# Start offsets of the on-chip tiles of a hybrid encoder block

## The chip, the cores and the metric

The kernel runs on one core of a Trainium2 chip. Its time is that of one execution on the device, in microseconds (us). The times shown are medians of several runs. A profile is a recording of one execution: for each engine of the core, what it executed and when. The engines are TensorE (PE in the profile; its weight loads are PEld), VectorE (DVE), ScalarE (ACT), GpSimd (POOL) and SyncE (SP), which here issues transfers.

## The reference

The reference is one encoder layer on 1,024 tokens of width 1,024, in float32:

```python
h   = x + concat[windowed_attention, bidirectional_gated_deltanet](RMSNorm(x) @ w_in) @ w_out
h   = h + square(relu(RMSNorm(h) @ w_ffn_in)) @ w_ffn_out
out = RMSNorm_final(h)
```

`w_in` has 2,832 columns: queries, keys and values of an attention with 8 query heads and 2 key heads of width 64 and a window of 128 tokens to each side, and queries, keys, values, gate and decay inputs of a gated DeltaNet with 4 heads of width 128, run forwards and backwards. The DeltaNet's queries, keys and values pass first through a centred convolution over 5 tokens and a SiLU. The feed-forward part has 4,096 inner columns.

## The kernel before

**Matmuls.** Large products are made of 128x512 matmuls: a 128x128 block of weights (the stationary operand) is loaded, and 512 columns (the moving operand) stream past it into one bank of PSUM. Each float32 operand is split into a rounded float32r part and the rest, and `mm3` (L122 to L126) issues three matmuls for each block: rounded by rounded, rounded by rest, rest by rounded. Lines 124, 125 and 126 are thus the three kinds of nearly all the matmuls. `split` (L116) makes the two parts, a cast on ScalarE (L119) and a subtraction on GpSimd or VectorE (L120).

**Stages.** The normalised input is transposed on TensorE and split into `pg` tiles. Then come eleven pairs of column blocks of `w_in` (`pair`, L263, with `gemm`, L257): weights in `wh` and `wl` tiles, moving operands in `pg`. The convolution reads raw projections from an `sc` tile (`proj_conv`, L380): 1,024 columns with two zero columns at each end. Beside the projections run the preparation and elimination of the DeltaNet's chunk matrices on VectorE. Then attention, the scan over chunks (`scan`, L768, small float32 matmuls in L797) and the output product (`out_gemm`, L869) are woven together. In `out_gemm` the weights are `pt` tiles and the moving operand is half a `w_out` row block, in `wh` and `wl` for three of the eight row blocks and in `pg` for five.

The feed-forward part computes block products with seven multiplications in place of eight. In the first product (`pair_products`, L1089, 16 groups of 7 products of 12 matmuls) the weights lie in `wh`, `wl` and `sc`, by a table (L1014), and the moving operands in `pg`. Its results go to memory from `pt` tiles (`sd`, L1077) and are read back into `pg` tiles (L1152). In the second product (`second_products`, L1178, four groups of seven steps, each of four banks of 12 matmuls) both operands are halves of `pg` tiles.

**Order.** Generators weighed against each other (`weave`, L55) fix the order of the program's instructions, and each engine executes its own in that order. Waits between engines come from the tiles: a tile that is given out anew waits for the last reader of its buffer.

**Where tiles lie.** A tile takes the same range of bytes in each of the 128 partitions. One pool, `const`, holds single tiles, and a second, `pool`, holds tags, each with its count of buffers (L88 to L110): 28 `pg`, 4 `sc`, 4 `wr`, 3 `wh`, 3 `wl` of 4,096 bytes (`sc` 4,112, because of the convolution's tile) and 12 `pt` of 2,048, and beside them the small tiles of `small`. `const` is opened first, so `pool` begins behind it, at whatever byte the constants end. In the program as built, the first free byte is 16,512 and each buffer takes a multiple of 32 bytes. `const` ends and `sc` begins at 23,648. The offsets from a multiple of 512 are then: `sc` 96, 128, 160 and 192 (its buffers are 4,128 bytes apart), `pg` and `wr` 224, `pt`, `wh` and `wl` 96 (small tiles of the tag `sm` lie in between). The last byte used is about 226,300.

Of the kernel before, what the change touches and what calls it, by code (L numbers as in the profile page):

```python
# [9 lines left out]
F32 = mybir.dt.float32  # L10
# [6 lines left out]
P = 128  # L17
SEQ = 1024
D = 1024
NT = SEQ // P  # L20
NK = D // P
HALF = 512
GH = 4
# [54 lines left out]
class Block:  # L78
# [28 lines left out]
        return self.buf("pt", 12, shape, dt)  # L107

    def small(self, shape, bufs=12, tag="sm", dt=F32):
        return self.buf(tag, bufs, shape, dt)  # L110

    def ps(self, tag, shape=(P, HALF)):
        return self.psum.tile(list(shape), F32, name=self.name(tag), tag=tag, bufs=4)
# [38 lines left out]
    def setup2(self):  # L152
        nc, io, c = self.nc, self.io, self.const
        t = lambda name, shape, dt=F32: c.tile(list(shape), dt, name=name)
        ones = t("ones", (P, P))
        nc.gpsimd.memset(ones, 1.0)
        self.ones = ones
        self.tri = []
        for d, (cm, step) in enumerate(((-1, 1), (1, -1))):
            u = t(f"tri{d}", (P, P))  # L160
            nc.gpsimd.affine_select(out=u, in_=ones, pattern=[[step, P]], compare_op=ALU.is_ge, fill=0.0,
                                    base=0, channel_multiplier=cm)
            self.tri.append(u)
        self.identb = t("identb", (P, P), BF16)
        nc.gpsimd.tensor_copy(out=self.identb, in_=self.ident)
        self.maskb = []
        for d in range(2):
            m = t(f"maskb{d}", (P, P), BF16)
            nc.gpsimd.tensor_scalar(out=m, in0=self.tri[d], scalar1=-1.0, scalar2=-NEG, op0=ALU.add, op1=ALU.mult)
            self.maskb.append(m)  # L170
        self.selb, self.zero = t("selb", (P, 16), BF16), t("zero", (P, 1))
        nc.gpsimd.memset(self.zero, 0.0)
        nc.gpsimd.tensor_tensor(out=self.selb, in0=self.ident[:, 0:16], in1=self.ident[:, 16:32], op=ALU.add)
        nc.gpsimd.tensor_tensor(out=self.selb, in0=self.selb, in1=self.ident[:, 32:48], op=ALU.add)
        self.dtb = t("dtb", (P, 8))
        nc.sync.dma_start(out=self.dtb, in_=io["gdn_dt_bias"].rearrange("o d h -> o (d h)").to_broadcast([P, 8]))
        self.alog = t("alog", (P, 8))
        nc.sync.dma_start(out=self.alog, in_=io["gdn_a_log"].rearrange("o d h -> o (d h)").to_broadcast([P, 8]))
        self.nsink = t("nsink", (P, 8))
        nc.sync.dma_start(out=self.nsink, in_=io["attn_sink"].to_broadcast([P, 8]))  # L180
        nc.gpsimd.tensor_scalar(out=self.nsink, in0=self.nsink, scalar1=-1.0, scalar2=None, op0=ALU.mult)
        self.ssk = t("ssk", (P, GH, NT))
        self.irk = t("irk", (P, GH, NT))
        self.rk2 = t("rk2", (P, GH, NT))
        self.ssq = t("ssq", (P, GH, NT))


# [192 lines left out]
    def proj_conv(self, c0, kind, raws=None):  # L380

        nc = self.nc
        for p in range(2):
            if raws is None:
                raws = self.load_w(self.w_cols(self.io["w_in"][0], c0 + 256 * p, 256))
            bufs = []
            for i, half, ps in self.pair(raws):
                if half == 0:
                    raw = self.sc((P, SEQ + 4))
                    nc.gpsimd.memset(raw[:, 0:2], 0.0)  # L390
                    nc.gpsimd.memset(raw[:, SEQ + 2:SEQ + 4], 0.0)
                    bufs.append(raw)
                raw = bufs[i]
                nc.scalar.copy(out=raw[:, 2 + half * HALF:2 + (half + 1) * HALF], in_=ps)
                yield 5.2
                if half == 1:
                    h = 2 * p + i
                    ct = {"q": 0, "k": 4, "v": 8}[kind] + h
                    out = None if kind == "v" else self.pg()
                    out = self.conv_silu(ct, raw, out)  # L400
                    getattr(self, "head_" + kind)(h, out)
            raws = None
# [832 lines left out]
    def build(self):  # L1235
        tc, nc = self.tc, self.nc
        with (
            tc.tile_pool(name="const", bufs=1) as self.const,
            tc.tile_pool(name="pool", bufs=1) as self.pool,
            tc.tile_pool(name="psum", bufs=1, space=bass.MemoryType.PSUM) as self.psum,  # L1240
            tc.tile_pool(name="dram", bufs=1, space=bass.MemoryType.DRAM) as dram,
        ):
            d = lambda name, shape: dram.tile(list(shape), F32, name=name)
            self.biasd = d("biasd", (8, 32, 512))[:]
            self.hd, self.sd = d("hd", (NT, P, D))[:], d("sd", (DFF // 256, 7, P, HALF))[:]
            self.gcd = dram.tile([3, 64, P], BF16, name="gcd")[:]
            self.zd, self.mad = d("zd", (GH, P, SEQ))[:], d("mad", (NT, P, HALF))[:]
            self.qad = d("qad", (2, 4, P, SEQ))[:]
            self.ktd, self.qtd = d("ktd", (GH, P, SEQ))[:], d("qtd", (GH, P, SEQ))[:]
            self.kvd = d("kvd", (NT, P, 2, GH, P))[:]  # L1250
            self.pd, self.atd = d("pd", (NT, P, 2, GH, P))[:], d("atd", (NT, P, 2, GH, P))[:]
            self.phases()
# [125 lines left out]
```

## Time and profile before

| | us |
|---|---|
| median of 3 runs | 1258.15 |
| lowest and highest | 1256.77 and 1258.52 |
| the profiled execution, span from first to last instruction | 1253.3 |

The profile gives no other time of the profiled execution than its span; the runs' times contain also what lies before its first and after its last instruction.

How to read its rows: in the page's groups, "L124 PE MATMUL psA<-pg,wh 128*128 128x512 f32 x416 | 167.6, 404" is line 124 on TensorE, writing `psA` from `pg` and `wh` (the two operands are not told apart by their order), 416 times, 167.6 us in all and 404 ns on average; then the idle time ahead of them and what ended it. Ends of matmuls in the records are modelled and overlap the next one's start, so the step from start to start is the time that one costs. The timeline gives start, duration, engine, line, operation and operands; neighbours of one kind are sometimes merged, with their count. Lists of transfers end in the size of one and the median time in us from issue to landing.

### The profile page before, as it was taken

How to read it: one execution, taken by the hardware profiler on the slowest of the kernel's cores; microseconds unless marked ns; L12 is line 12 of the kernel's file. 1: busy time of each engine (PE TensorE's matmuls, PEld its weight loads, DVE VectorE, ACT ScalarE, POOL GpSimd, SP SyncE). 2: the span in 40 equal slices, each digit the busy share in tenths (PEclk: the TensorE clock that was granted, in tenths of full speed). 3: DMA queues.
4: the chain of work that ended last, by engine and by line, in shares of the span. 5: the costliest groups of instructions: out<-in, count | busy, mean ns of one | idle time of the engine just before them, and what ended most of it. 6: DMA issues, size and time to landing. Idle time of an engine off the chain costs nothing.

```text
span 1253.3 us, 18527 instructions
## 1 busy us (share of the span) xinstructions
PE 1191.6 (95%) x6482; PEld 967.2 (77%) x6482; DVE 854.9 (68%) x1528; ACT 621.4 (50%) x1347; POOL 580.3 (46%) x488
## 2 busy tenths in 40 slices
PE   7999999899789989998999999999999999999997
PEld 5778777677568868877788888888777888888885
DVE  5667667982389986676655454544668797886976
ACT  6455688335485752125464554545545434444343
POOL 5354211362432433144573534535445665655595
PEclk9999999899889999998999999999999999999999
DMA  7134344441956678122234344443678624434323
GB/s 239 52 121 133 101 171 140 139 126 40 223 168 158 190 216 296 60 84 85 84 131 159 132 151 143 154 159 134 223 280 280 223 85 167 151 121 148 95 90 135
DMA packets 121630, 187.62 MB, mean 150 GB/s; under 512 B 11043, under 2 KB 64416, under 8 KB 121537
## 3 DMA queue, kind: packets, MB, share of 16 engines
q1 hardware_dynamic: 96708, 152.58, 37.9%
q10 hardware_dynamic: 16381, 29.67, 6.3%
q0 software_dynamic: 8448, 4.20, 1.9%
q8 instruction: 51, 0.84, 0.3%
q14 instruction: 42, 0.34, 0.1%
HBM read 122.39 MB, written 63.49 MB: 148 GB/s over the span
## 4 chain that ended last, share of the span: by engine, by line
PE 49%; DVE 6%; DMA 3%; issue 2%; POOL 1%; ACT 1%; ACTq 0%; POOLq 0%; DVEq 0%; SPq 0%
PE psA L124 8%; PE psA L125 8%; PE psA L126 8%; PE psB L126 7%; PE psB L125 7%; PE psB L124 7%; DMA pg<-sd 3%; PE psB L797 2%; DVE pg L1154 1%; DVE pt L1163 1%; DVE wr L1166 1%; PE psB L209 1%; DVE pg L1199 1%; DMA sd<-pt 0%; DVE wr L1161 0%
## 5 line engine op out<-in xcount | busy, mean ns | idle before, releaser
L124 PE MATMUL psA<-pg,wh 128*128 128x512 f32 x416 | 167.6, 404 | 2.1 <-ACT pt L458 2.1
L126 PE MATMUL psA<-pg,wl 128*128 128x512 f32 x416 | 166.9, 401 | 0.0
L125 PE MATMUL psA<-pg,wh 128*128 128x512 f32 x416 | 166.5, 400 | 0.0
L120 POOL TENSOR_TENSOR wl<-wr,wh 128x512 fp32r<-128x512 f32 x44 | 70.2, 1618 | 154.0 <-ACT wh L119 153.9
L1154 DVE TENSOR_TENSOR pg<-pg 128x512 fp32r<-128x512 f32 x112 | 122.7, 1127 | 18.8 <-ACT pg L1153 18.6
L120 POOL TENSOR_TENSOR wh<-wr,wh 128x512 fp32r<-128x512 f32 x32 | 47.9, 1518 | 131.5 <-ACT wh L119 131.5
L1071 ACT ACTIVATE pt<-pt 128x512 f32<-128x512 f32 x64 | 40.4, 632 | 122.7 <-DVE pt L1061 122.7
L125 PE MATMUL psA<-pg,pg 128*128 128x512 f32 x256 | 99.7, 391 | 0.5 <-POOL pg L120 0.5
L124 PE MATMUL psA<-pg,pg 128*128 128x512 f32 x256 | 99.0, 391 | 1.0 <-DVE pg L1199 1.0
L126 PE MATMUL psA<-pg,pg 128*128 128x512 f32 x256 | 99.7, 389 | 0.0
L120 POOL TENSOR_TENSOR pg<-wr,pg 128x512 fp32r<-128x512 f32 x48 | 73.4, 1560 | 51.0 <-ACT pg L119 51.0
L124 PEld LDWEIGHTS psA<-pg,wh 128*128 128x128 f32 x416 | 79.2, 190 | 21.3 <-ACT pt L458 2.4
L125 PEld LDWEIGHTS psA<-pg,wh 128*128 128x128 f32 x416 | 79.3, 191 | 19.7 <-issue 0.9
L126 PEld LDWEIGHTS psA<-pg,wl 128*128 128x128 f32 x416 | 79.1, 190 | 18.6
L1153 ACT CAST pg<-pg 128x512 fp32r<-128x512 f32 x112 | 67.2, 620 | 41.3 <-DMA pg<-sd 31.0
L126 PE MATMUL psB<-pg,pg 128*128 128x512 f32 x192 | 75.0, 390 | 1.3 <-DVE pg L1154 1.3
L125 PE MATMUL psB<-pg,pg 128*128 128x512 f32 x192 | 75.0, 391 | 0.8 <-POOL pg L120 0.7
L124 PE MATMUL psB<-pg,pg 128*128 128x512 f32 x192 | 74.7, 390 | 0.4 <-ACT pg L1153 0.4
L119 ACT CAST wh<-wr 128x512 fp32r<-128x512 f32 x76 | 43.6, 623 | 45.5 <-PE psA L125 24.8
L1061 DVE TENSOR_TENSOR pt<-psB,pt 128x512 f32<-128x512 f32 x39 | 26.9, 689 | 55.1 <-PE psB L126 30.1
L1061 DVE TENSOR_TENSOR pt<-psA,pt 128x512 f32<-128x512 f32 x39 | 26.8, 689 | 55.0 <-PE psA L126 39.5
L124 PEld LDWEIGHTS psA<-pg,pg 128*128 128x128 f32 x256 | 48.0, 188 | 12.6 <-DVE pg L1199 2.3
(385 smaller groups left out, 3307.7 us busy)
## 6 DMA issues: line engine op xcount, KB each, us to landing
sd<-pt ACTq DMA_DIRECT2D x112, 256.0 KB, 2.2
pg<-sd SPq DMA_DIRECT2D x112, 256.0 KB, 2.9
wr<-in_w_ffn_in SPq DMA_DIRECT2D x32, 512.0 KB, 3.8
wr<-in_w_in SPq DMA_DIRECT2D x22, 512.0 KB, 4.8
pg<-in_x SPq DMA_DIRECT2D x16, 512.0 KB, 5.4
wr<-in_w_ffn_out SPq DMA_DIRECT2D x16, 512.0 KB, 4.8
sc<-kvd SPq DMA_DIRECT2D x14, 512.0 KB, 4.1
kvd<-pt SPq DMA_DIRECT2D x16, 256.0 KB, 2.8
```

Source lines behind the costliest of these rows:

```text
L119: nc.scalar.copy(out=h, in_=raw)
L120: (eng or nc.gpsimd).tensor_tensor(out=l, in0=raw, in1=h.bitcast(F32), op=ALU.subtract)
L124: nc.tensor.matmul(ps, wh, xh, start=first, stop=False, skip_group_check=onto)
L125: nc.tensor.matmul(ps, wh, xl, start=False, stop=False, skip_group_check=onto)
L126: nc.tensor.matmul(ps, wl, xh, start=False, stop=last, skip_group_check=onto)
L209: self.nc.tensor.transpose(ps[:, i * P:(i + 1) * P], row[:, k * P:(k + 1) * P], self.ident)
L797: nc.tensor.matmul(ps[:, h - g.start, :], left(h), right[:, h, :], start=True, stop=True)
L1061: self.nc.vector.tensor_tensor(out=out, in0=in0, in1=in1, op=ALU.add)
L1071: self.nc.scalar.activation(out=c, in_=c, func=AF.Relu)
L1153: nc.scalar.copy(out=s[:, 0], in_=raw)
L1154: v.tensor_tensor(out=s[:, 1], in0=raw, in1=s[:, 0].bitcast(F32), op=ALU.subtract)
L1163: v.tensor_tensor(out=b["T2"], in0=b["B22"], in1=b["T1"], op=ALU.subtract)
```

## The change

The pool `pool` is opened ahead of `const`, behind a new pool `head` that holds three tiles of 128 bytes taken out of `const`: 16,512 + 384 = 16,896 = 33 x 512. The convolution's tile is 1,152 columns (4,608 bytes) instead of 1,028, of which the same 1,028 are used; as the largest tile of its tag it sets the size of the four `sc` buffers. Small tiles go to a pool `few` behind the constants. So `pool` holds only buffers of 4,096, 4,608 and 2,048 bytes, and each begins at a multiple of 512. Instructions, their engines, counts of buffers and transfers are the same.

```diff
     def small(self, shape, bufs=12, tag="sm", dt=F32):
-        return self.buf(tag, bufs, shape, dt)
+        return self.few.tile(list(shape), dt, name=self.name(tag), tag=tag, bufs=bufs)
...
-        self.ssk = t("ssk", (P, GH, NT))
-        self.irk = t("irk", (P, GH, NT))
-        self.rk2 = t("rk2", (P, GH, NT))
+        self.ssk, self.irk, self.rk2 = (self.head.tile([P, GH, NT], F32, name=n) for n in ("ssk", "irk", "rk2"))
...
-                    raw = self.sc((P, SEQ + 4))
+                    raw = self.sc((P, SEQ + P))
...
         with (
+            tc.tile_pool(name="head", bufs=1) as self.head,
+            tc.tile_pool(name="pool", bufs=1) as self.pool,
             tc.tile_pool(name="const", bufs=1) as self.const,
-            tc.tile_pool(name="pool", bufs=1) as self.pool,
+            tc.tile_pool(name="few", bufs=1) as self.few,
```

## The prediction

> **What bounds the kernel now.** The page comes first, for the span and the engine that is busy.
>
> ```profile
> span 1253.3 us, 18527 instructions
> PE 1191.6 (95%) x6482; PEld 967.2 (77%) x6482; DVE 854.9 (68%) x1528; ACT 621.4 (50%) x1347; POOL 580.3 (46%) x488
> PE   7999999899789989998999999999999999999997
> PEclk9999999899889999998999999999999999999999
> PE 49%; DVE 6%; DMA 3%; issue 2%; POOL 1%; ACT 1%; ACTq 0%; POOLq 0%; DVEq 0%; SPq 0%
> ```
>
> TensorE is busy 95% of the span, at nearly the full granted clock, and the chain of waits gives it 49%, against 3% for DMA. (Its shares do not add up to 100% because matmuls overlap in the records.) Next come the stretches: start and end, the length, then busy time and count for each engine, the granted clock, the DMA share and GB/s.
>
> ```profile
> 16.00:194.00 178.00, 176.82 (x866) 141.10 (x865) 122.52 (x195) 108.37 (x304) 64.60 (x64) 1.00 0.38 118
> 194.00:288.00 94.00, 87.81 (x456) 69.84 (x454) 71.85 (x178) 48.08 (x99) 31.79 (x24) 0.96 0.40 129
> 288.00:470.00 182.00, 162.86 (x1717) 132.35 (x1716) 131.39 (x412) 110.53 (x285) 63.24 (x61) 0.95 0.63 171
> 470.00:580.00 110.00, 106.04 (x586) 90.48 (x585) 71.57 (x188) 25.67 (x76) 36.55 (x32) 0.98 0.40 140
> 622.00:892.00 270.00, 267.97 (x1153) 215.18 (x1152) 137.12 (x185) 140.59 (x249) 137.65 (x105) 1.00 0.41 143
> 892.00:948.00 56.00, 51.31 (x212) 40.41 (x211) 35.92 (x47) 26.62 (x47) 23.10 (x16) 0.97 0.80 275
> 948.00:1253.00 305.00, 294.20 (x1285) 239.87 (x1283) 248.90 (x276) 130.06 (x231) 191.07 (x133) 0.99 0.45 148
> ```
>
> In the projections' first part (16 to 194) and in the first feed-forward product (622 to 892) TensorE is busy over 99% while each other engine is at 69% or less. There, time is the number of matmuls times their spacing. Their spacing is therefore the thing to look at, and "busy" hides it, since a record lasts longer (390 to 404 ns) than the step from one start to the next.
>
> **The spacing depends on where operands lie.** The timeline gives each matmul's start. Below are the first and last starts of unbroken runs, all 128x512 float32r.
>
> ```profile
> 477.00 0.39 PE L126 MATMUL psA<-wh,pt 128*128 128x512 f32 x1
> ...
> 478.36 0.39 PE L126 MATMUL psA<-wh,pt 128*128 128x512 f32 x1
> ...
> 720.86 0.39 PE L124 MATMUL psA<-pg,sc 128*128 128x512 f32 x1
> ...
> 723.67 0.40 PE L126 MATMUL psB<-pg,sc 128*128 128x512 f32 x1
> ...
> 728.30 0.39 PE L124 MATMUL psB<-pg,sc 128*128 128x512 f32 x1
> ...
> 731.09 0.40 PE L124 MATMUL psB<-pg,wh 128*128 128x512 f32 x1
> ...
> 732.08 0.39 PE L124 MATMUL psA<-pg,wh 128*128 128x512 f32 x1
> ...
> 739.51 0.40 PE L126 MATMUL psB<-pg,wl 128*128 128x512 f32 x1
> ...
> 740.45 0.40 PE L124 MATMUL psB<-pg,sc 128*128 128x512 f32 x1
> ...
> 743.25 0.39 PE L126 MATMUL psA<-pg,sc 128*128 128x512 f32 x1
> ...
> 745.54 0.39 PE L126 MATMUL psB<-pg,wl 128*128 128x512 f32 x1
> ...
> 1023.70 0.39 PE L124 MATMUL psB<-pg,pg 128*128 128x512 f32 x1
> ...
> 1029.14 0.39 PE L124 MATMUL psB<-pg,pg 128*128 128x512 f32 x1
> ```
>
> Read with the byte offsets of the program as built, modulo 512 (pg and wr 224; pt, wh and wl 96; the four sc buffers 96, 128, 160 and 192, because each takes 4,112 bytes):
> - weights and moving operand both at 224: 24 steps from 1023.70 to 1029.14, 226.7 ns each;
> - both at 96 (out_gemm): 6 steps from 477.00 to 478.36, 226.7 ns;
> - weights 128 bytes before the moving operand's offset, in wh and wl: 32 steps from 732.08 to 739.51, 232.2 ns; the same in sc at 96: 12 steps from 728.30, 232.5 ns;
> - weights in sc at 128: 12 steps from 720.86, 234.2 ns; at 192: 12 steps from 740.45, 233.3 ns; at 160: 10 steps from 743.25, 229.0 ns.
>
> Four sc buffers in one stage, under the same load on the other engines, give three different spacings; equal offsets give 226.7 in two different stages. So the spacing follows the difference of the two operands' offsets, and zero is the best of the five differences seen. After the change every pg, wr, sc, wh, wl and pt tile starts at 0, and operands inside them at multiples of 512: all differences become zero.
>
> **The change part by part.** No instruction is added, taken away or given to another queue; only addresses change.
>
> Matmuls with unequal offsets: 11 projection pairs of 96 make 1,056; in out_gemm 240 of 384 (those whose w_out halves are pg tiles against pt weights); the first feed-forward product has 16 groups x 7 products x 12 = 1,344. That is 2,640. The second product's 1,344 and 144 of out_gemm are equal already. The runs in wh and wl (232.2) and the mean of the four sc runs (232.2) agree, so each of the 2,640 should lose 232.2 - 226.7 = 5.5 ns, 14.5 us in all. What of it reaches the end:
> - projections, 1,056 x 5.5 ns = 5.8 us. TensorE is busy 99%, 93% and 89% in the stretches they lie in; where it waits, VectorE's convolution and elimination are late instead and keep part of the gain. I take 85%: 4.9 us.
> - out_gemm, 240 x 5.5 ns = 1.3 us, woven with the scan, whose chain alternates between TensorE and VectorE. Half: 0.7 us.
> - first feed-forward product, 1,344 x 5.5 ns = 7.4 us, nearly all under a busy TensorE. No engine behind it is near its limit (ScalarE 141 and GpSimd 138 of 270 us), so nothing is late next until its last groups, where loads end the waits. 95%: 7.0 us.
>
> Sum 12.6 us. From the rows alone this sum lies between 0 (offsets do nothing) and 14.5 us. The second product gains nothing from the difference.
>
> The other engines' operations:
>
> ```profile
> L119 ACT CAST wh<-wr 128x512 fp32r<-128x512 f32 x76 | 43.6, 623 | 45.5 <-PE psA L125 24.8 <-issue 18.4 <-DVE wr L1036 1.5
> L119 ACT CAST sc<-wr 128x512 fp32r<-128x512 f32 x31 | 19.0, 612 | 4.9 <-DVE wr L1044 2.3 <-PE psA L126 1.3 <-PE psB L126 1.3
> L120 POOL TENSOR_TENSOR wl<-wr,wl 128x512 fp32r<-128x512 f32 x31 | 40.9, 1341 | 3.4 <-ACT wl L119 3.4
> L120 POOL TENSOR_TENSOR sc<-wr,sc 128x512 fp32r<-128x512 f32 x31 | 40.9, 1320 | 1.3 <-ACT sc L119 1.3
> ```
>
> The cast into sc, at four offsets, takes 612 ns and into wh, at one, 623; the subtraction 1,320 and 1,341. Differences of 2% on engines at half load cost nothing on the path, so I take zero; both lie under the matmuls. Small tiles in a pool of their own keep their count of buffers, so no new wait arises. The padded convolution tile is still written and read in its first 4,112 bytes, and the layout still fits on chip (four tiles grow by 496 bytes each), so no transfer is added.
>
> DMA:
>
> ```profile
> wr<-in_w_ffn_out SPq DMA_DIRECT2D x16, 512.0 KB, 4.8
> sc<-in_w_ffn_out SPq DMA_DIRECT2D x8, 512.0 KB, 4.7
> wh<-in_w_ffn_out SPq DMA_DIRECT2D x4, 512.0 KB, 4.4
> ```
>
> The same load lands in 4.8 us at offset 224, 4.7 in sc and 4.4 at 96. Queues explain that as well as addresses do. If it were all address, 0.4/4.8 = 8% of DMA's 3% of the span (37.6 us) is 3.1 us; the other bound is zero, since the bytes stay the same. I take zero, as the start of a load is set by what was issued ahead of it, and keep 3 us for the low end. [...]
>
> The sum is made on the profiled execution: span 1253.3 - 12.6 = 1240.7. The three times lie 3.5 to 5.2 us over that span, the median 4.85 us, which is start and end around it. Forecast: 1258.15 - 12.6 = **1245.5 us**.
>
> **The rivals.**
>
> *Offsets are not the cause, nothing changes* (1258). For it: most of the 226.7 matmuls stand in one stage and most of the 232 ones in others. Against it: the run at 477.00 and the run in sc at 743.25 (229.0), each in a stage of slower ones. [...]
>
> *The good rhythm is not kept after pauses* (1252). Equal offsets do not always run at 226.7:
>
> ```profile
> L124 PE MATMUL psA<-wh,pt 128*128 128x512 f32 x48 | 19.1, 397 | 0.0
> L124 PE MATMUL psA<-pg,pg 128*128 128x512 f32 x256 | 99.0, 391 | 1.0 <-DVE pg L1199 1.0
> ```
>
> Those at 96 in out_gemm average 397 ns of record, those at 224 391, and they alternate with unequal ones. If short pauses break the rhythm, half of the 12.6 us comes: 1252. Against it: the second product pauses too, and its average is 391.
>
> *Multiples of 512 are a bad common place* (slower). No pair in this trace starts at a multiple of 64; both good cases are 32 past one. If both streams starting on a boundary meet on the same rows of the memory at every fetch, all 4,128 could take the worst spacing seen, 234.2: 2,640 x 2.0 + 1,488 x 7.5 ns = 16.4 us, nine tenths of it on the path, 1273. It decides from a common spacing of (2,640 x 232.2 + 1,488 x 226.7)/4,128 = 230.2 ns upward. Against it: moving from 224 to 96 cost nothing.
>
> *Starting on a boundary also removes what is left at zero difference* (much faster).
>
> ```profile
> 383.82 1.47 PE L573 MATMUL psA<-ident,wr 128*128 128x128 f32 x12
> ...
> 399.78 0.49 PE L573 MATMUL psA<-ident,wr 128*128 128x128 f32 x3
> ```
>
> Twelve plain float32 transposes take 1.47 us and three take 0.49, so one steps by 0.98/9 = 109 ns for 128 columns. If float32r streams at twice that rate, 512 columns need 218 ns: 8.7 ns less than 226.7, over 4,128 matmuls 35.9 us, 85% of it 30.5, and the time 1215. [...] Against it: weights at 128 and 192, multiples of 64, are among the slowest. [...]
>
> **How the numbers follow.** Forecast 64%, rhythm lost 8%, nothing 8%, slower 7%, much faster 13%. The likeliest gives 1245.5, its own range 1240 to 1250 (all of the 14.5 us with DMA's 3, down to two thirds). The range 1236 to 1258 leaves out the last two cases, 20%. About 0.2%, 2.5 us, is what a measurement of this kernel can tell from none; faster is 64 + 8 + 13 = 0.85, the same 0.08, slower 0.07.
>
> **What the new profile would show.** Unbroken runs step by 226 to 227 ns with weights in wh, wl, sc and pg alike, and their records fall from 400 ns to 390; a group of the first feed-forward product, now 19.6 us (731.56 - 711.94),
>
> ```profile
> 711.94 0.49 PE L124 MATMUL psB<-pg,sc 128*128 128x512 f32 x1
> ...
> 731.56 0.45 PE L124 MATMUL psA<-pg,sc 128*128 128x512 f32 x1
> ```
>
> takes about 19.1; the second product keeps its 226.7, and the casts their 612 to 623 ns. A second product at 230 or more shows the slow rival; one near 218 shows the fast one; sc and wh runs that stay at 232 show that the difference of offsets was not the cause. Steps of 227 with an unchanged end would mean that waits on VectorE and loads take the gain, and that my shares of 85 to 95% were wrong.

## The result, and the profile after

| | us |
|---|---|
| before, median (lowest, highest) of 6 runs | 1257.62 (1256.4, 1259.99) |
| after, median (lowest, highest) of 6 runs | 1248.93 (1246.77, 1253.05) |
| ratio after to before, 95% interval | 0.9933, 0.9918 to 0.9949 |
| the profiled execution after, and its span | 1248.56, 1246.8 |

The change made the kernel 0.7% faster: 8.7 us between the medians, 6.5 us between the spans of the two profiled executions. Forecast were 12.6. The page of the kernel after opens with the span and the engines' busy time:

```profile
span 1246.8 us, 18527 instructions
PE 1184.7 (95%) x6482; PEld 968.6 (78%) x6482; DVE 854.8 (69%) x1528; ACT 620.7 (50%) x1347; POOL 577.9 (46%) x488
```

Counts of instructions are the same, and the other engines' busy time hardly moves. Two of the stretches of the kernel after (start and end, length, busy time and count of PE, PEld, DVE, ACT and POOL, granted clock, DMA share, GB/s):

```profile
16.00:194.00 178.00, 176.52 (x880) 142.87 (x879) 124.56 (x197) 109.33 (x307) 63.56 (x64) 1.00 0.37 119
...
622.00:892.00 270.00, 270.00 (x1167) 219.67 (x1167) 132.19 (x180) 138.60 (x245) 137.99 (x104) 0.99 0.42 148
```

In the same 270 us of the first feed-forward product TensorE now begins 1,167 matmuls where it began 1,153. That is 1.2% more; a step of 227 ns for 232 would give 2.3%. Its granted clock there is 0.99 where it was 1.00. In the projections (16 to 194 us) it is 880 for 866, or 1.6%. The second row already says that half of this stage's gain went somewhere.

The timeline of the kernel after, first and last starts of unbroken runs (weights in `sc`, and in the second product in `pg`), then the first matmuls of two successive groups of the first product, the same two whose distance the prediction shows:

```profile
718.16 0.39 PE L124 MATMUL psA<-pg,sc 128*128 128x512 f32 x1
...
720.65 0.39 PE L126 MATMUL psA<-pg,sc 128*128 128x512 f32 x1
...
1018.10 0.39 PE L124 MATMUL psB<-pg,pg 128*128 128x512 f32 x1
...
1023.54 0.39 PE L124 MATMUL psB<-pg,pg 128*128 128x512 f32 x1
```

```profile
709.41 0.50 PE L124 MATMUL psB<-pg,sc 128*128 128x512 f32 x1
...
728.73 0.50 PE L124 MATMUL psA<-pg,sc 128*128 128x512 f32 x1
```

The run in `sc` steps by 2.49/11 = 226.4 ns and the second product by 5.44/24 = 226.7, as before. A group takes 19.32 us: 19.62 before, 19.1 forecast.

The other engines and the loads after (busy time and mean of one; for the load, the median time from issue to landing):

```profile
L119 ACT CAST sc<-wr 128x512 fp32r<-128x512 f32 x31 | 19.0, 612 | 5.9 <-DVE wr L1042 2.3 <-PE psB L126 2.3 <-PE psA L126 1.3
L120 POOL TENSOR_TENSOR sc<-wr,sc 128x512 fp32r<-128x512 f32 x31 | 40.5, 1308 | 2.8 <-ACT sc L119 2.8
...
wr<-in_w_ffn_out SPq DMA_DIRECT2D x16, 512.0 KB, 5.1
```

The cast takes 612 ns as before, the subtraction 1,308 for 1,320, and the load 5.1 us at offset 0 for 4.8 at 224. Where the time went shows in the starts of the same matmuls in both timelines:

| matmul (start, us) | before | after | gained so far |
|---|---|---|---|
| one late in the projections | 278.5 | 274.9 | 3.6 |
| one of the projections, 7 us later | 285.1 | 283.0 | 2.1 |
| first of `out_gemm` | 473.5 | 470.8 | 2.7 |
| first of the first feed-forward product | 606.7 | 603.0 | 3.7 |
| last of the first feed-forward product | 950.5 | 944.0 | 6.5 |
| last of the program | 1244.3 | 1238.1 | 6.2 |

### The profile page after: what moved, and what is told of

It reads as the page before. It is cut to its first block, busy times and chain, and to the rows that moved or that the text cites. A ratio compares the mean times of both kernels' runs of the same rounds, so it can differ in the third digit from the quotient of the medians.

```text
span 1246.8 us, 18527 instructions
## 1 busy us (share of the span) xinstructions
PE 1184.7 (95%) x6482; PEld 968.6 (78%) x6482; DVE 854.8 (69%) x1528; ACT 620.7 (50%) x1347; POOL 577.9 (46%) x488
```

## The experiments

Ratios are to the kernel before, measured in the same series. "The feed-forward part" is the time from the start of its first matmul to the start of the program's last one: 637.6 us before, 635.1 after, by the table above.

**The changed kernel once more.** No edit; it gives the spread between series.

> The changed kernel once more, beside the others on the same chip. Expected 1249 us, 8 to 9 us less than the kernel before, and float32r runs that step by 226 to 227 ns in all stages. The theory on the throttle (a half-clock stretch of 6.8 us at 620 us took about 2.8 us of the gain in the first profile) expects that stretch to move or to be missing in some profiles; if it stands at 620 us again, it belongs to this layout.

Measured: 1248.95 us (1247.18 to 1249.77), ratio 0.9914 (0.9886 to 0.9942), span 1247.8. The feed-forward part takes 635.9 us. The gain holds. The half-clock stretch of which the expectation speaks stands in this profile too, from 620.4 us on; an experiment below says why that does not make it a property of the layout.

**The kernel before once more**, in one execution, for its span and its clock.

> The kernel before, profiled a second time. Theory (the changed layout brings a half-clock stretch at about 620 us, since its faster filler matmuls leave TensorE idle for most of one interval of the clock's control): here TensorE keeps the full clock from 600 to 640 us, as in its first profile. Rival (that stretch comes and goes by chance in either kernel): half clock at 620 us here too.

Measured: 1256.17 us with a span of 1254.4, feed-forward part 637.2 us, full clock around the start of the first feed-forward product. The time lies 1.8 us above the span, as after (1248.56 - 1246.8). The prediction read the 4.85 us between its profile's span and the median as start and end. Only some 1.8 of them were; that profiled execution was itself about 3 us faster than that median.

**All large tiles at 224.** Is it the boundary, or only that the offsets are equal?

```diff
+        self.head.tile([P, 56], F32, name="shift")
```

> The changed layout with a further tile of 224 bytes in front, so that all large tiles begin 224 bytes past a multiple of 512, with equal offsets. Theory (only the difference of the offsets counts): steps of 226 to 227 ns in all stages and the time of the changed kernel, 1249 us, within 0.2%. Rival (the beginning at a multiple of 512 itself counts): steps over 228 ns and 1252 us or more.

The 224 bytes shift every large tile from 0 to 224. The timeline of this kernel, a run in `sc`:

```profile
721.74 0.39 PE L124 MATMUL psA<-pg,sc 128*128 128x512 f32 x1
...
724.24 0.39 PE L126 MATMUL psA<-pg,sc 128*128 128x512 f32 x1
```

Eleven steps of 2.50/11 = 227 ns, as at 0. Measured: 1251.44 us (1248.17 to 1255.56), ratio 0.9933 (0.9908 to 0.9957), whose interval overlaps that of the changed kernel in the same series. The boundary does nothing for TensorE's steps; equality does it. The time is 2.5 us above that of the changed kernel, at the edge of what the expectation allows. Where it goes was not tried; the profiled execution, the slowest of the eight, has half-clock stretches at 409 and 959 us that neither profile of the changed kernel has.

**The convolution's tile without its padding.** The four `sc` buffers then lie at 0, 32, 64 and 96 and the moving operand at 128; `wh` and `wl` stay equal to `pg`.

```diff
-                    raw = self.sc((P, SEQ + P))
+                    raw = self.sc((P, SEQ + 4))
```

> The changed layout without the padded convolution tile: the sc buffers begin at 0, 32, 64 and 96, every other large tile at 128, so only weights in sc have unequal offsets (differences of -128, -96, -64, -32, as before the change). Theory: wh, wl, pt and pg runs stay at 226 to 227 ns, sc runs are back at 229 to 234, on the mean 232; 576 matmuls times 5.5 ns are 3.2 us, so about 1251 to 1252 us. Rival (the sc tiles do not matter for the end because the first feed-forward product waits on ScalarE's casts anyway): 1249 us, the same as the changed kernel.

The timeline of this kernel, a run in `sc` and one in `wl`:

```profile
725.91 0.40 PE L124 MATMUL psB<-pg,sc 128*128 128x512 f32 x1
...
728.47 0.40 PE L126 MATMUL psB<-pg,sc 128*128 128x512 f32 x1
...
735.21 0.39 PE L124 MATMUL psB<-pg,wl 128*128 128x512 f32 x1
...
737.70 0.40 PE L126 MATMUL psB<-pg,wl 128*128 128x512 f32 x1
```

The run in `sc` is back at 2.56/11 = 232.7 ns, the one in `wl` stays at 226.4. In one stage and under one load, only the runs whose offsets differ are slow. Measured: 1251.43 us (1248.92 to 1253.08), ratio 0.9934 (0.9912 to 0.9956). That is 2.5 us above the changed kernel in the same series. The 576 matmuls with weights in `sc` at 6 ns make 3.5; but the intervals overlap, and the kernel at 224, with all its steps fast, took as long in this series (1251.44). So the steps prove the effect, and the time can neither prove nor refute it.

**A map of differences.** `sc`, `wh` and `wl` in pools of their own behind gaps, the convolution's tile unpadded. Against the moving operand at 0 the weights lie at 256 (`wh`), 64 (`wl`) and 128, 160, 192 and 224 (`sc`).

```diff
+        pool = {"sc": self.pool_sc, "wh": self.pool_sc, "wl": self.pool_wl}.get(tag, self.pool)
...
+        self.gap1.tile([P, 32], F32, name="gap1")
+        self.gap2.tile([P, 80], F32, name="gap2")
```

> The changed layout with pg, wr and pt at 0 (modulo 512), wh at 256, wl at 64 and the four sc buffers at 128, 160, 192 and 224, so that five new differences between weights and moving operand stand in one execution. Theory (spacing is a function of the difference modulo 512, zero alone gives 226.7): every run of wh, wl and sc steps by 229 to 235 ns. Rival (modulo 256 or 128 is enough): wh runs at 226 to 227 ns, and sc at 128 too under modulo 128. The time should lie at that of the kernel before, 1256 to 1260 us, under the theory.

The timeline of this kernel: runs at 256, 64 and 160.

```profile
715.14 0.39 PE L127 MATMUL psA<-pg,wh 128*128 128x512 f32 x1
...
717.18 0.39 PE L127 MATMUL psA<-pg,wh 128*128 128x512 f32 x1
...
717.88 0.40 PE L125 MATMUL psA<-pg,wl 128*128 128x512 f32 x1
...
720.45 0.39 PE L127 MATMUL psA<-pg,wl 128*128 128x512 f32 x1
720.68 0.40 PE L125 MATMUL psA<-pg,sc 128*128 128x512 f32 x1
...
723.24 0.39 PE L127 MATMUL psA<-pg,sc 128*128 128x512 f32 x1
```

The steps are 226.7 at 256 (9 steps), 233.6 at 64 (11) and 232.7 at 160 (11); over all runs, 128 gives 232.9, 192 gives 230.7 and 224 gives 233.1. So 256 is as good as 0, once a run has gone on for a while; over all runs of `wh` the mean was 229.1, because many of them follow a break. The time, 1253.85 us in one execution with a span of 1252.1, lies below the expected 1256 to 1260. Not all runs of `wh` were slow, as the expectation had them; one execution says no more.

**`sc` at 0 and 256.** The map suggests that the difference counts modulo 256.

```diff
-                    raw = self.sc((P, SEQ + P))
+                    raw = self.sc((P, SEQ + 64))
```

> After the change, with the convolution's tile padded to 4,352 bytes (17 x 256) in place of 4,608: the four sc buffers then begin at 0, 256, 0 and 256 modulo 512, everything else at 0. Theory (the spacing follows the difference of the operands' offsets modulo 256, as the runs in wh at a difference of 256 suggest, which step by 226.7 ns once they have run for a while): sc runs step by 226.7 at both offsets, the first feed-forward product's mean step is 227 as after the change, and the time is that of the changed kernel, 1248 to 1250. Rival (it follows the difference modulo 512, and 256 is a middling value, 229 ns as the mean of all runs at 256): the sc runs in the two buffers at 256 step by 229 to 230, the mean of this product is near 228, the time 1249 to 1251.

The timeline of this kernel, an `sc` run at 256 (`sc` buffers alternate; which one it is was read from the program as built):

```profile
735.10 0.39 PE L124 MATMUL psB<-pg,sc 128*128 128x512 f32 x1
...
737.59 0.39 PE L126 MATMUL psB<-pg,sc 128*128 128x512 f32 x1
```

Eleven steps of 226.4 ns, the mean of the product 227.1, and of all steps with weights in `sc` 227.0. Measured: 1248.56 us (1247.77 to 1251.7), ratio 0.9939 (0.9923 to 0.9955): the changed kernel's time. Padding to a multiple of 256 is enough here, and the rival with 512 falls.

**Where the first feed-forward product's gain went: the clock.** The timeline of TensorE around the start of the tokens' last transposes (L209 before, L207 after), before and then after; brackets give the wait and what ended it:

```profile
619.58 1.04 PE L209 MATMUL psB<-ident,sc 128*128 128x128 f32 x8
621.65 0.63 PE L209 MATMUL psB<-ident,sc 128*128 128x128 f32 x4 [1.04 <-DVE pt L993]
623.62 0.63 PE L209 MATMUL psB<-ident,sc 128*128 128x128 f32 x4 [1.34 <-DVE pt L993]
624.94 0.47 PE L124 MATMUL psB<-pg,wh 128*128 128x512 f32 x1 [0.69 <-DVE pt L1002]
```

```profile
615.63 1.03 PE L207 MATMUL psB<-ident,sc 128*128 128x128 f32 x8
617.93 0.63 PE L207 MATMUL psB<-ident,sc 128*128 128x128 f32 x4 [1.26 <-DVE pt L991]
619.90 0.63 PE L207 MATMUL psB<-ident,sc 128*128 128x128 f32 x4 [1.35 <-DVE pt L991]
621.22 0.77 PE L124 MATMUL psB<-pg,wh 128*128 128x512 f32 x1 [0.69 <-DVE pt L1000]
621.78 0.63 PE L125 MATMUL psB<-pg,wh 128*128 128x512 f32 x1
...
626.48 0.63 PE L124 MATMUL psB<-pg,wl 128*128 128x512 f32 x1
```

In both, the early products run out and TensorE waits three times for VectorE. After it, the new kernel's matmuls step by (626.48 - 621.78)/11 = 427 ns instead of 227: the granted clock is halved from 620.5 to 627.3 us, and some 14 matmuls lose 2.8 us. The edit that tests it gives TensorE more to do while it waits: the last two blocks of transposes are done three times, with the same results (16 transposes more; the first expectation speaks of six blocks, the edit does it for two).

```diff
-    def token_block(self, rows, k):
+    def token_block(self, rows, k, times=1):
...
+        for _ in range(times):
...
-            ps = self.token_block(rows, 4 + k)
+            ps = self.token_block(rows, 4 + k, 3 if k > 1 else 1)
```

> The changed layout, with the transposes of six of the sixteen token blocks ahead of the first feed-forward product written two or three times over: 4 to 8 additional transposes of 109 ns in each of the last blocks, so that TensorE has less idle time from 614 to 621 us. They leave the result as it is. Theory (low activity in one interval brings the half clock in the next two): no half-clock stretch at 620 us, the first group's matmuls step by 227 ns instead of 427, and about 2.8 us come back, less up to 2 us that the additional transposes delay VectorE's chain; 1247 to 1249 us. Rival (half clock comes at this place whatever TensorE does before): the stretch stays and the time is 1250 to 1251.

> After the change, with the last two blocks of the token transposes done three times and nothing else: the control for the kernel that has the cast's order besides. Theory: 1246 to 1248, no half clock at 620 us. Rival (the 2 us that it gained over the changed kernel were spread between runs): 1249 to 1250.

> The kernel before, with the last two blocks of the token transposes done three times (16 more transposes in all). Theory (the transposes pay only where they keep TensorE's clock from falling, and before the change it does not fall at this place): they lie in time in which TensorE idles, so 1256 to 1259, ratio 1.000 within 0.2%; then offsets together with the transposes are worth some 10 us. Rival (the transposes help by themselves, whatever the offsets): 1254 to 1255.

Measured: 1247.15 us (ratio 0.9925, 0.9902 to 0.9948) and 1248.46 us (0.9915, 0.99 to 0.9929); no half clock at this place in either profile, feed-forward part 633.5 and 634.0 us, so 1.1 to 2.4 less than in the two profiles of the changed kernel. The kernel before with the same edit takes 1257.41 us, ratio 0.9985 (0.9971 to 0.9998), feed-forward part 637.2 us as in its second profile. The interval just leaves out 1, so a small gain is there too. As times, 1247.15 and 1248.46 are not separated from the changed kernel's 1248.93 and 1248.95, nor are the ratios.

Apart from the one at the program's end, every half-clock stretch in these traces lasts 3.4, 6.8 or 10.2 us, and within one trace all of them lie on one raster of 3.41 us; against the program's start the raster lies elsewhere in each trace. The views below show stretches cut on each trace's own raster. The columns are as above; after the length come PE's busy time and count, and the granted clock stands third from the end. First before:

```profile
619.50:622.90 3.40, 1.74 (x13) 1.22 (x11) 3.40 (x7) 2.42 (x4) 3.22 (x4) 1.00 0.00 0
622.90:626.30 3.40, 1.99 (x10) 1.59 (x11) 2.92 (x5) 2.79 (x6) 2.70 (x3) 1.00 0.00 0
```

after:

```profile
617.10:620.50 3.40, 1.23 (x8) 0.84 (x8) 3.40 (x7) 1.92 (x4) 2.52 (x3) 1.00 0.00 0
620.50:623.90 3.40, 2.71 (x7) 2.15 (x7) 2.92 (x5) 3.40 (x7) 3.40 (x3) 0.50 0.00 0
```

after, with more transposes:

```profile
615.90:619.30 3.40, 2.10 (x18) 1.93 (x19) 3.40 (x7) 1.93 (x4) 2.52 (x3) 1.00 0.00 0
```

and the kernel with `sc` at 0 and 256, whose instructions are those of the changed kernel:

```profile
615.90:619.30 3.40, 1.85 (x14) 1.31 (x12) 3.40 (x6) 2.38 (x5) 3.23 (x4) 1.00 0.00 0
619.30:622.70 3.40, 1.66 (x9) 1.31 (x10) 2.92 (x6) 2.63 (x6) 2.69 (x3) 1.00 0.00 0
```

A period with 1.23 us of work is followed by half clock; periods with 1.66, 1.74, 1.85 and more are not. The last kernel has the same waits as the changed one and keeps its clock, because a line of the raster falls into the middle of the idle time and halves it (feed-forward part 633.8, as with more transposes). So my first reason, that the faster early products leave a longer wait, falls: the three waits make 3.1 us before and 3.3 after, and where the raster cuts them decides. The half clock came here in both profiles of the changed kernel, in those of the kernels at 224, without the padding and with P5's cast first, and in the map, where most steps are slow, each time behind a period with 0.9 to 1.4 us of work. It did not come in the two profiles of the kernel before.

That was the luck of the raster. If a period of 3.41 us is slid along the trace, the least work that it holds at this place is 1.03 us before, 0.81 after, and 1.66 with more transposes in either of their profiles. So the kernel before can lose its clock here as well: its 1.03 us lie below the 1.23 that were followed by half clock after the change. With the transposes no place of the raster holds less than 1.66, which kept the clock in the kernel with `sc` at 0 and 256. The clocks of all executions point the same way. In one series the mean granted clock was 0.9812 over 17 executions of the kernel before, 0.9833 over 12 of it with more transposes, and 0.9833 over 6 of the changed kernel with them. A stretch at half clock lowers the mean by half of its share, so the 0.0021 are an estimate of 5 us less at half clock in 1257, give or take 2. So the kernel before, too, seems to lose its clock here in many executions, perhaps most, and the half clock explains the difference between the two profiles and not that between the medians.

What sets the raster's place stays open.

Over all periods of the 14 traces from 15 us on, one at full clock with less than 1.59 us of work was always followed by half clock, one with more than 2.05 never. So a period need not be idle to cost the clock: 1.23 us of work in it still cost it at 620 us after the change.

**The second loss: a cast, once a group.** The timeline around the start of a group, before and then after (ScalarE's casts of P6's weights, from `wr`, and of P5's, from `pt`, then TensorE's weight load, which waits for the second; after, also the activation that opens this stretch of ScalarE's queue):

```profile
691.19 0.60 ACT L119 CAST sc<-wr 128x512 fp32r<-128x512 f32 x1
691.70 0.61 ACT L119 CAST sc<-pt 128x512 fp32r<-128x512 f32 x1
...
692.36 0.19 PEld L124 LDWEIGHTS psA<-pg,sc 128*128 128x128 f32 x1 [0.19 <-ACT sc L119]
```

```profile
686.70 0.63 ACT L1069 ACTIVATE pt<-pt 128x512 f32<-128x512 f32 x1 [0.90 <-DVE pt L1059]
...
688.88 0.60 ACT L119 CAST sc<-wr 128x512 fp32r<-128x512 f32 x1
689.39 0.62 ACT L119 CAST sc<-pt 128x512 fp32r<-128x512 f32 x1
...
690.06 0.19 PEld L124 LDWEIGHTS psA<-pg,sc 128*128 128x128 f32 x1 [0.40 <-ACT sc L119]
```

Before, the cast arrived about as TensorE needed it. Now TensorE comes 0.2 us too early, in eleven groups one after another, from 690 to 884 us. Between 627 and 890 us the steps over 245 ns exceed 227 by 0.7 us in all before and by 2.75 after. The cast of P5's weights stands in ScalarE's queue behind that of P6's, and both behind the activation that waited 0.90 us for VectorE; from there ScalarE works without a pause. The edit moves the cast of P5 ahead of that of P6:

```diff
-        take("P6", "P5", "P7", "P3", "P4")
+        take("P5", "P6", "P7", "P3", "P4")
```

> The changed layout, but each group of the first feed-forward product makes its weights of the step P5 ahead of those of P6, so that the cast of P5, for which TensorE waits once a group, no longer stands behind the cast of P6 in ScalarE's queue. Theory (this wait ate the gain of the first product: a group takes 19.33 us instead of 84 x 226.8 ns = 19.05): a group takes 19.05 to 19.12 us, and with 14 groups the time is about 3 us less, 1246 us. Rival (the wait only moves to another cast or another bank): a group stays at 19.3 us and the time at 1249.

Measured: 1249.77 us (1249.04 to 1252.38), ratio 0.9926 (0.9898 to 0.9954). Nine of ten groups take 19.06 to 19.11 us, as the theory had it, and one 19.86. The excess from 627 to 890 us falls to 0.8, and that from 890 to 945 rises from 6.6 to 11.3, of which 2.0 are matmuls at half clock behind the wait. The waits of TensorE and of ScalarE at the end of the product in this kernel (who waits for what: total, times, longest):

```profile
PE psA L124 <- ACT pt L1064: 4.5, 1, 4.5
...
ACT pg L1151 <- DMA pg<-sd: 8.3, 1, 8.3
```

ScalarE's queue is held by a cast that waits 8.3 us for a load (`pg` from memory, for the second product), and the copy that TensorE needs stands behind it. The 2 us won went into another wait, as the rival had it for the time.

**Both together**, with the old order kept for the last group:

```diff
+        take(*(("P6", "P5") if last else ("P5", "P6")), "P7", "P3", "P4")
...
+                cols[g + 1] = self.columns(self.load_w1(g + 1), 0, g + 2 == ng)
```

> After the change, with the last two blocks of the token transposes done three times (their results are the same) and the cast of P5's weights ahead of P6's in every group but the last. Theory (two separate losses in the first feed-forward product: the half clock at its start, and a wait on ScalarE's cast once a group; the order at the last group is what moved the wait to 893 us before): both losses go, the product's groups take about 19.2 us in place of 19.33, its gaps fall from 5 us to about 2.5, nothing grows at 890 to 910, and the time is about 2.4 us below the kernel with more transposes alone: 1244 to 1246. Rival (the end of this stage is set by loads, so that a faster product only waits longer there): the product is faster by the same 2.4 us but the wait at 890 to 945 takes it, and the time stays at 1247 to 1248.

> The kernel with more transposes and P5's cast ahead in all groups but the last, once more, to see whether it holds its time: 1244 to 1247 if both losses are real, 1248 to 1250 if its lower time was spread between runs.

Measured: 1245.84 us (1243.38 to 1249.11), ratio 0.9903 (0.9887 to 0.9919), and 1245.23 us (1243.02 to 1248.32), ratio 0.9908 (0.9889 to 0.9926): the lowest times of this study. In the same series they lie 2.6 us below the kernel with more transposes alone and 3.3 us below that with `sc` at 0 and 256, though the intervals still overlap. The feed-forward part takes 632.3 and 632.1 us. Ten groups take 191.7 and 191.5 us for 193.3 after the change. The theory was half right: a part of that is given back behind these groups, where the excess from 890 to 945 us is 10.0 and 10.1 for 6.6. From its first to its last matmul the product takes 338.8 and 338.6 us, with more transposes alone 339.5 and 340.2. One wait of ScalarE in the second profile:

```profile
ACT pg L1152 <- DMA pg<-sd: 7.5, 1, 7.5
```

The load still holds ScalarE's queue at the end of the product, with the last group's order unchanged; so that order is not what moved the wait, against the expectation. That this load sets the stage's end is the likeliest reading; no run moves the load.

## Why the prediction was right, and where its steps were not

**The cause.** The spacing follows the difference of the two operands' offsets: right. It was undone in `sc` alone and came back there alone. At a common 224 no step is longer (227 ns in `sc`, as at 0), so both rivals about the boundary (1273 and 1215) fall: the second product steps by 226.7 at 0 as it did at 224. That offsets do nothing falls too: with the same instructions at other addresses, the run in `sc` at 718.16 us steps by 226.4 ns, where those before stepped by 229.0 to 234.2.

**5.5 ns for each of 2,640 matmuls.** In the first feed-forward product the mean of all steps up to 245 ns fell from 232.4 to 227.1, in `out_gemm` from 231.1 to 228.2, in the projections from 232.6 to 227.9. Of the 384 in `out_gemm`, though, 144 were equal before; behind the 240 others the step fell from 232.1 to 228.0. So 5.3 of the 5.5 came in the long runs and 4.1 to 4.7 in the others. The rival about pauses was right in part, and the timeline after shows it, behind a break:

```profile
610.84 0.39 PE L124 MATMUL psA<-pg,wh 128*128 128x512 f32 x1
...
612.00 0.39 PE L126 MATMUL psA<-pg,wh 128*128 128x512 f32 x1
...
612.68 0.39 PE L126 MATMUL psA<-pg,wh 128*128 128x512 f32 x1
...
615.40 0.39 PE L126 MATMUL psA<-pg,wl 128*128 128x512 f32 x1
```

The first five steps take 232 ns each, the last twelve 226.7. Over the whole trace, steps 1 to 4 behind a break average about 231 ns, the next four 229, the next four 227.5, later ones 226.7. Why a run needs about twelve matmuls to find its rhythm was not tried.

**Projections, 4.9 us; `out_gemm`, 0.7.** In the first pair of profiles 3.6 us had been gained at 278.5 us. Then the kernel after runs at half clock from 279.2 to 282.6, where the kernel before does not, and 2.1 us are left (columns as in the stretches above):

```profile
279.20:282.60 3.40, 3.40 (x49) 2.75 (x38) 0.02 (x1) 2.98 (x6) 0.00 (x0) 0.50 0.02 5
```

At the start of `out_gemm` it is 2.7 us and at that of the feed-forward part 3.7, against 5.6 forecast; `out_gemm` thus gave 1.0 for 0.7. In the second pair (each kernel once more) it is the kernel before that runs at half clock there, from 283.2 us on, and the gains are 4.0 and 5.3. So most of the missing 1.9 us is the luck of the clock. The smaller step makes about 0.8 (1,056 matmuls by 0.8 ns); what share the waits keep cannot be told from two pairs.

**First feed-forward product, 95% of 7.4 us: the step that failed.** It gained 6.5 - 3.7 = 2.8 us, and 2.6 in the second pair of profiles. The spacing gave 1,344 x 5.3 ns = 7.1; in these profiles the half clock took 2.8 and the casts 2.75 - 0.7 = 2.0, which leaves 2.3. The prediction said that no engine behind it is near its limit, "so nothing is late next". That was read from ScalarE's total of 141 us in 270. The order in its queue and the moment at which one cast comes free made it late by 0.2 us a group all the same. And nothing in the working asked how near TensorE's idle time at 620 us was to costing the clock: 1.74 of 3.4 us, as the stretches show. That explains the profiles. Between the medians, 12.6 - 8.7 = 3.9 us are missing; if the kernel before loses its clock there as often, the half clock is no part of them. By the profiles the casts are 2.0 and the projections' smaller step 0.8; the rest stays open.

**Zeros.** The casts (612 ns), the subtractions (1,308 for 1,320) and the second product: right. DMA at zero: right, the load of 4.8 us takes 5.1 after, 4.2 in the kernel with all large tiles at 224, and that of `pg` from memory 2.9 in all of them.

**The sum.** 12.6 us forecast; 6.2 to 6.6 in the two pairs of profiles, 8.7 between the medians. The forecast of 1245.5 is 3.4 us low, inside its own range of 1240 to 1250, and the direction was right. That the range holds is owed to its width: of the largest term, 7.0 us, 2.8 came in the profiles. The 4.85 us around the span were really 1.8.

## What to carry to other kernels

Where matmuls follow one another without waits, read their step from start to start and sort it by the byte offsets of both operands: here every pair whose offsets agreed modulo 256 ran at 226.7 ns once the run had gone on for a while, every other at 229 to 234, so tiles padded to multiples of 256 bytes were enough. A gain in a stage that is "99% busy" still has to pass the next queue: look at how long before its use each operand is ready (here 0 to 0.2 us), not at the busy share of the engine that makes it. And cut the idle stretches of TensorE into pieces of 3.4 us: here every one with less than 1.59 us of work lost the clock behind it, at 620 us for 6.8 us, and whether a piece held so little depended on where the raster lay. With 16 transposes in the idle time the piece shown above held 2.10 us, and the clock stayed. Before a stage's gain is read from one pair of profiles, compare where each was at half clock.

## What was not expected of the hardware

- Offsets of weights and moving operand: differences of 0 and 256 gave 226.4 to 227 ns for 512 columns of float32r; in the map, 64 gave 233.6, 128 gave 232.9, 160 gave 232.7, 192 gave 230.7 and 224 gave 233.1; before the change, 384 gave 232.2 and 232.5, 416 gave 234.2, 448 gave 229.0 and 480 gave 233.3. The offset that both share (0, 96, 224) made no difference: 226.4 to 227 ns at each.
- A run starts, on average, at about 231 ns after a break and settles at 226.7 only after about twelve matmuls.
- The granted clock changed on a raster of 3.41 us that kept its place within each of the 14 traces and lay elsewhere in the next; at 620 us a period with 1.23 us of work was followed by two periods at half clock, one with 1.66 by none. The same waits of 3.3 us cost 2.8 us or nothing, by where the raster divided them.
